# One reading of w_out: block sums in the conv output's place, and the first left sum kept in SBUF

## The chip, the cores and the metric

The kernel runs on one core of a Trainium2 chip. The metric is the device time of one execution in microseconds. Engines are named as in the profile: PE is TensorE (matmul), PEld its weight load, DVE is VectorE, ACT is ScalarE, POOL is GpSimd, SP is SyncE, which issues nearly all of the DMAs and issues them in order. "wo" is the program's name for the PSUM banks of the product with w_out.

## What is computed

One layer of a hybrid decoder: batch 1, 1024 tokens, width 1024, all in fp32. The part that matters here is its middle:

```
c   = silu(layer_norm(conv(...)))
y_b = c @ w_proj_conv
g_a, g_b = split(sigmoid(g + gate_b))
x   = x + (g_a * y_a + g_b * y_b) @ w_out        # w_out is 1024 x 1024
h   = rms_norm(x) * ffn_norm_w
x   = x + (silu(h @ w_gate) * (h @ w_up)) @ w_down
```

The attention branch gives y_a ahead of this. With m = g_a * y_a + g_b * y_b, the stage that is changed is x + m @ w_out, together with the projection with w_proj_conv just before it, in which m is made.

## The kernel before

**Precision.** Each fp32 operand is split into a high part (a cast on ScalarE, `split_hi`, L120) and a low part (a subtraction on VectorE, `split_lo`, L125). A product takes three matmuls: high x high, high x low, low x high. Weights come through `wraw` (two buffers of 128x1024) into `whi` and `wlo` (three buffers of each). A `Stream` (`ws`) holds the list of the loads and splits; `ws.next()` hands out the next weight and sees to it that up to two more are begun.

**The product with w_out.** It is done in seven products of half size, not eight, in Winograd's form of Strassen's method. m is cut into four blocks: token half by even or odd 128-row tile of the contraction. w_out is cut in four: W11, W12, W21, W22, by the even or odd 128-row tile (first digit) and by column half (second digit). The sums are

```
left:   S1 = m21 + m22    S2 = S1 - m11    S3 = m11 - m21    S4 = m12 - S2
right:  T1 = W12 - W11    T2 = W22 - T1    T3 = W22 - W12    T4 = W21 - T2
```

and the products are 11 (m11 W11), 12 (m12 W21), S2 T2, S1 T1, S4 W22, S3 T3, 22 (m22 T4). A product has four contraction tiles j, four row tiles i and three matmuls for each, 48 matmuls of 128x128 by 128x512. They go into three groups of four PSUM banks called a, b and c. Group b (two `pm`, two `pg` banks) takes 11, S2, S3 and 22 one on top of the other. Group a takes 12, group c takes S1 and then S4; a and c use the same four `pw` banks. After each product VectorE adds its banks to the rows of x (`xa`, L1786), which are loaded by `x_rows` (L1744), and only then may a bank be written again.

**Where the operands come from.** In the conv projection (loop over groups of channel tiles `(0,1,2), (3,4), (5,6), (7,)`, token half `sb`, channel tile c) every turn loads a gate (`gt<-g_d`, L1619, eight slots) and a row block of the attention branch (`ya`, L1672), multiplies (L1674), adds (L1675) and splits the result into `mT_hi`, `mT_lo` (all but the block m21, whose place stays empty). After each odd c in the second half, `side_sums` (L552 to L558) makes the four left sums of a pair of channel tiles and stores them in HBM (`so`). Between the turns `weight_sums` (L533 to L544) loads w_out in pieces of 128x512 (2 x 256 columns of two row tiles), makes the four right sums of each piece with four subtractions of 128x256 (L539 to L542) and stores them in HBM (`to`). In the w_out stage the S-products load a left sum and its right operand side by side into one 128x1024 buffer, and split both at once (`ld_seven`: L447, L449, L452); the others load two blocks of w_out or T4 (`ld_two`, L500). The buffers of S2, S1 and S4 are rows of the two large tiles that held the conv output (`rooms`, tags xhi and xlo), which are free once the last conv matmul has read them; the rest goes through `wraw`.

**What sets the order.** Each engine and each DMA queue works in order. The order is made by the framework's planner, which simulates the program with estimated durations and puts what it expects to be ready first, by the order of the program. `with after(ins)` puts what follows behind `ins` on the queue of its engine. So the loads of the S2, S1 and S4 operands and of the x rows stand behind the last DMA issued on SP at that point:

```
            if z == 0 and j == 0:
                with after(last_of(mybir.EngineType.SP)):
                    for step in wo_steps["S2"]:
                        step.load()
                    x_rows(0)
                    for step in wo_steps["S1"]:
                        step.load()
                    x_rows(1)
```

The norm weights of the channel mixer (`fnw_b`, L1703) are loaded by ScalarE's queue and scaled on VectorE (L1732) in the same stage. The transposes of the first token half's normed rows (`norm2`) go in between the matmuls of the last two products, and write into the large tiles (`h2_hi`, `h2_lo`).

Of the kernel before, what the change touches and what calls it, by code (L numbers as in the profile page):

```python
# [57 lines left out]
def kernel(  # L58
# [224 lines left out]
    def wraw():  # L283
        return wp.tile([P, 1024], F32, tag="wraw", name=nm("wraw"), bufs=2)
# [104 lines left out]
    so = {z: [dr.tile([P, 512], F32, name=f"so{z}_{j}") for j in range(NKT // 2)] for z in SIDES[3:]}  # L389
    to = {z: [dr.tile([P, 512], F32, name=f"to{z}_{j}") for j in range(NKT // 2)] for z in SUMS}  # L390
# [46 lines left out]
    WSEVEN = tuple(SEVEN[z] for z in (0, 1, 2, 3, 5, 4, 6))  # L437

    def ld_seven(n, sides, w, sums, raw_tile, which=SEVEN):


        def step(a_, b_, j):
            raw = []

            def load():
                raw.append(raw_tile())
                nc.sync.dma_start(raw[0][:, :512], sides[a_][j][:])  # L447
                if b_ in sums:
                    nc.sync.dma_start(raw[0][:, 512:], sums[b_][j][:])  # L449
# [12 lines left out]
        return [step(a_, b_, j) for a_, b_, _, _, _ in which for j in range(n)]  # L462
# [26 lines left out]
    def ld_two(b_, q):  # L489

        def go():
            raw = wraw()
            for e in range(2):
                j = 2 * q + e
                if b_ in to:
                    src = to[b_][j][:]
                else:
                    r0 = (2 * j + b_[0]) * P
                    src = wout[r0 : r0 + P, 512 * b_[1] : 512 * (b_[1] + 1)]
                nc.sync.dma_start(raw[:, 512 * e : 512 * (e + 1)], src)  # L500
            hi, lo = wsplit(raw)
            return hi[:].rearrange("p (k c) -> p k c", c=512), lo[:].rearrange("p (k c) -> p k c", c=512)

        return go

    rooms = []

    def wo_raw():
        if rooms:
            return rooms.pop(0)  # L510
        return wraw()

    wo_steps = {}
    for e_ in WSEVEN:
        if e_[0][0] == "S":
            wo_steps[e_[0]] = ld_seven(NKT // 2, so, wout, to, wo_raw, (e_,))
        else:
            wo_steps[e_[0]] = [ld_two(e_[1], q) for q in range(2)]
        ws.plan(wo_steps[e_[0]])
# [29 lines left out]
    def side_sums(a11, a21, a12, a22, s1, dst, s3=None):  # L549
# [7 lines left out]
        for z, t_ in (("S1", s1), ("S2", a11), ("S4", a21)):  # L557
            nc.sync.dma_start(dst[z], t_[:])  # L558
# [908 lines left out]
    yp_ctx = ExitStack()  # L1467

    def y_tiles(n):
        yp = yp_ctx.enter_context(tc.tile_pool(name=f"yp{n[0]}", bufs=1, side="right", reuse_waits="tile"))  # L1470
        return lambda name: [
            [yp.tile([P, S], F32R, tag=f"y{z}{k}", name=f"{name}{z}{k}") for k in n]
            for z in ("h", "l")
        ]
# [182 lines left out]
    def wo_tiles():  # L1657
        b = bs.tile([P, 2, 2, 256], F32, tag="wd", name=nm("wd"), bufs=2)
        return [b[:, 0], b[:, 1]]

    osum = weight_sums(NKT // 2, wout, to, wo_tiles, 256)
    osum[0][0]()
    M = {}
    nturn = 0
# [72 lines left out]

    for z, tag in enumerate(("xhi", "xlo")):
        room = f32(big.tile([P, NKT, S], F32R, tag=tag, name=f"room{z}")[:])
        rooms.extend(room[:, k, :] for k in range(NKT if z == 0 else 4))  # L1740
# [7 lines left out]
    for z, (z_, b_, s_, (l, c), full) in enumerate(WSEVEN):  # L1748
        if z == 5:
            h2_hi = big.tile([P, NKT, S], F32R, tag="xhi", name="h2_hi")  # L1750
            h2_lo = big.tile([P, NKT, S], F32R, tag="xlo", name="h2_lo")
# [3 lines left out]
        for j in range(4):  # L1755
            if z_[0] == "S" or j % 2 == 0:
                hi, lo = ws.next()
            if z == 0 and j == 0:
                with after(last_of(mybir.EngineType.SP)):
                    for step in wo_steps["S2"]:  # L1760
                        step.load()
                    x_rows(0)
                    for step in wo_steps["S1"]:
                        step.load()
                    x_rows(1)
                    for step in wo_steps["S4"]:
                        step.load()
            for i in range(4):
                t_ = slice(i * P, (i + 1) * P)
                if z_[0] == "S":  # L1770
                    A, B = [m_[:, t_] for m_ in (hi, lo)], [m_[:, 512:] for m_ in (hi, lo)]
                else:
                    k, cs = 2 * j + int(z_[1]) - 1, TOK[int(z_[0]) - 1]
                    A, B = [m_[k][:, cs][:, t_] for m_ in (mT_hi, mT_lo)], [m_[:, j % 2, :] for m_ in (hi, lo)]
# [284 lines left out]
```

## Time and profile before

| what | value |
|---|---|
| median of 3 runs | 1753.03 us (1752.62 to 1755.97) |
| the profiled execution | 1756.5 us |
| its span on the core | 1754.7 us |
| TensorE busy in the span | 1726.1 us, 98% |
| VectorE, ScalarE, GpSimd busy | 1284.9, 864.1, 210.7 us |
| mean granted TensorE clock | 0.994 |
| HBM read, written | 184.99 MB, 86.54 MB |

The profile is of one execution. Its span runs from the first to the last instruction on the core, and the rows below give times from the span's start. In the rows of groups the numbers are: count, busy us in total, mean ns of one, idle us of the engine before them and what ended that idle time. In rows of the timeline: start, duration, engine, line, operation. In the chain of waits: start, duration, what the time went to. "DMA share" is the mean busy share of 16 DMA engines. The conv projection lies at about 924 to 1013 us, the w_out stage at 1013 to 1106 us.

### The profile page before, as it was taken

The numbers are of one execution on the slowest core, as the hardware profiler recorded it, in microseconds if no ns is written. First come the engines' busy times: TensorE is split into PE (matmuls) and PEld (weight loads), VectorE is DVE, ScalarE is ACT, GpSimd is POOL, SyncE is SP. The second block draws the span as 40 slices with busy tenths as digits, with TensorE's granted clock in tenths as the row PEclk, the third lists the DMA queues.
The fourth block names the chain that finished last, engine by engine and source line by source line (L and its number), as shares of the span: only waits on it lengthen the run. The fifth ranks groups of instructions, "written<-read, shape, count | busy, mean of one in ns | idle before, by whom it ended". The sixth has DMA issues, their size and how long they took to land.

```text
span 1754.7 us, 26010 instructions
## 1 busy us (share of the span) xinstructions
PE 1726.1 (98%) x9245; PEld 1482.7 (84%) x9245; DVE 1284.9 (73%) x2156; ACT 864.1 (49%) x1956; POOL 210.7 (12%) x199
## 2 busy tenths in 40 slices
PE   9999999999999999999999989999999999999999
PEld 7997889998998999987787867788888888888887
DVE  7575889998987988886777756967667666565544
ACT  5333435677776786755465224643333333333332
POOL 4987851000000000000000000000000000000000
PEclk9999999999999999999999989999999999999999
DMA  6343455234244344335855894334545544598663
GB/s 204 115 132 115 156 177 162 75 103 149 81 121 139 105 112 124 115 112 182 298 193 162 276 336 162 108 102 155 169 150 162 179 152 143 165 352 294 216 216 132
DMA packets 267591, 289.52 MB, mean 165 GB/s; under 512 B 17282, under 2 KB 187330, under 8 KB 267460
## 3 DMA queue, kind: packets, MB, share of 16 engines
q1 hardware_dynamic: 265184, 281.08, 50.0%
q0 software_dynamic: 1840, 5.19, 1.0%
q8 instruction: 73, 1.20, 0.3%
q10 hardware_dynamic: 436, 1.58, 0.2%
q14 instruction: 58, 0.48, 0.1%
HBM read 184.99 MB, written 86.54 MB: 155 GB/s over the span
## 4 chain that ended last, share of the span: by engine, by line
PE 85%; DVE 6%; DMA 5%; ACT 2%; issue 1%; SPq 0%; DVEq 0%; ACTq 0%
PE acc L977 29%; PE acc L482 12%; PE pg L168 10%; PE pg L169 10%; PE pg L170 10%; PE sc L1286 2%; PE sc L1285 2%; PE wo L1776 2%; PE pT L1324 2%; DVE acc L596 1%; PE pW L169 1%; PE pW L168 1%; PE pW L170 1%; DMA soS<-gt 1%; PE pg L1103 1%
## 5 line engine op out<-in xcount | busy, mean ns | idle before, releaser
L596 DVE SCALAR_TENSOR_TENSOR acc<-u,cw,acc 128x1023 f32<-128x1023 f32 (+14 forms) x240 | 303.5, 1265 | 12.5 <-ACT acc L590 10.0
L168 PE MATMUL pg<-whi,hT_hi 128*128 128x256 f32 x704 | 199.9, 285 | 0.5 <-DVE v L125 0.5
L170 PE MATMUL pg<-whi,hT_lo 128*128 128x256 f32 x704 | 199.8, 284 | 0.0
L169 PE MATMUL pg<-wlo,hT_hi 128*128 128x256 f32 x704 | 199.4, 284 | 0.0
L125 DVE TENSOR_TENSOR wlo<-draw,whi 128x1024 fp32r<-128x1024 f32 x75 | 91.8, 1223 | 84.1 <-ACT whi L120 76.5
L120 ACT CAST whi<-draw 128x1024 fp32r<-128x1024 f32 x75 | 79.1, 1055 | 129.5 <-PE acc L482 117.6
L120 ACT CAST whi<-wraw 128x1024 fp32r<-128x1024 f32 x98 | 102.9, 1052 | 77.7 <-PE pg L169 33.7
L168 PEld LDWEIGHTS pg<-whi,hT_hi 128*128 128x128 f32 x704 | 133.9, 191 | 2.2 <-DVE v L125 0.7
L169 PEld LDWEIGHTS pg<-wlo,hT_hi 128*128 128x128 f32 x704 | 134.2, 191 | 1.8
L170 PEld LDWEIGHTS pg<-whi,hT_lo 128*128 128x128 f32 x704 | 134.2, 191 | 1.7
L482 PE MATMUL acc<-wlo,whi 128*128 128x512 f32 x308 | 119.8, 389 | 0.0
L482 PE MATMUL acc<-whi,wlo 128*128 128x512 f32 x308 | 119.8, 389 | 0.0
L125 DVE TENSOR_TENSOR wlo<-wraw,whi 128x1024 fp32r<-128x1024 f32 x83 | 102.3, 1234 | 19.2 <-ACT whi L120 18.6
L168 PE MATMUL pg<-hT_hi,whi 128*128 128x512 f32 x288 | 114.5, 398 | 0.1
L169 PE MATMUL pg<-hT_lo,whi 128*128 128x512 f32 x288 | 114.1, 396 | 0.0
L170 PE MATMUL pg<-hT_hi,wlo 128*128 128x512 f32 x288 | 113.7, 395 | 0.0
L1292 ACT ACTIVATE E<-E,mn 128x640 f32<-128x640 f32 (+7 forms) x128 | 99.7, 779 | 23.1 <-DVE mn L1287 22.6
L120 ACT CAST whi<-s 128x1024 fp32r<-128x1024 f32 x54 | 56.8, 1052 | 107.6 <-PE acc L977 103.8
L1287 DVE CUSTOM_DVE_ANT_0 E<-sc,tb 128x512 f32<-128x512 f32 (+3 forms) x128 | 74.2, 585 | 27.6 <-PE pT L1324 13.7
L977 PE MATMUL acc<-h_hi,whi 128*128 128x512 f32 x240 | 93.4, 389 | 0.0
L977 PE MATMUL acc<-h_lo,whi 128*128 128x512 f32 x240 | 93.4, 389 | 0.0
L977 PE MATMUL acc<-h_hi,wlo 128*128 128x512 f32 x240 | 90.1, 389 | 0.0
(349 smaller groups left out, 4583.6 us busy)
## 6 DMA issues: line engine op xcount, KB each, us to landing
wraw<-in_w_gate_up_dram SPq DMA_DIRECT2D x44, 512.0 KB, 4.8
wraw<-in_w_in_dram SPq DMA_DIRECT2D x40, 512.0 KB, 4.6
qs<-qs SPq DMA_DIRECT2D x96, 128.0 KB, 2.3
wd<-in_w_down_dram SPq DMA_DIRECT2D x44, 256.0 KB, 3.2
tdT<-wd SPq DMA_DIRECT2D x88, 128.0 KB, 4.7
draw<-sdS SPq DMA_DIRECT2D x44, 256.0 KB, 3.7
draw<-tdT SPq DMA_DIRECT2D x44, 256.0 KB, 3.9
wraw<-in_w_in_dram SPq DMA_DIRECT2D x32, 256.0 KB, 3.3
```

Of the source, the lines that this page charges most:

```text
L120: act.copy(dst, src)
L125: last_lo[0] = dve.tensor_tensor(dst, src, f32(hi), op=ALU.subtract).ins
L168: pe.matmul(o, lh, rh, start=start, stop=False)
L169: pe.matmul(o, lh, rl, start=False, stop=False)
L170: last_mm[0] = pe.matmul(o, ll, rh, start=False, stop=stop).ins
L482: m = pe.matmul(o[s_][i][:], l_[:, ts], r_[:, 512:], start=start and j + y_ == 0, stop=j == n - 1 and y_ == 2, skip_group_check=not start,)
L596: dve.scalar_tensor_tensor(a_, us[c][:, : S - n], cw[:, c, t : t + 1], a_, op0=ALU.mult, op1=ALU.add)
L977: last_mm[0] = pe.matmul(o[:], a_[x_][:, k, :], b_[y_][:, k, :], start=start and k + x_ + y_ == 0, stop=k == 3 and x_ == 1, skip_group_che ...
L1285: pe.matmul(o[:, :w], qh[:, qs], k, start=True, stop=False)
L1286: last_mm[0] = pe.matmul(o[:, :w], ql[:, qs], k, start=False, stop=True).ins
L1287: dve.tensor_tensor_reduce(e[:, ks], o[:, :w], tb[:, S - nk + c0 : S - nk + c0 + w], 1.0, mn[:, j : j + 1] if c0 else 3.0e38, ALU.add, ALU ...
L1292: act.activation(e[:, :nk], e[:, :nk], AF.Exp, bias=mn[:, j : j + 1], scale=-1.0, accum_out=l[:, j : j + 1])
```

## The change

Five things change, all in these two stages.

1. `weight_sums` for w_out leaves the conv projection, with its tiles, its loads, its subtractions and its stores; `to` is gone.
2. `side_sums` no longer stores S1. The conv projection splits it at once into the empty place of m21 in `mT_hi` and `mT_lo`, and the S1 product takes its left operand there.
3. At the start of the w_out stage W21, W12, W11 and W22 are loaded in one piece (`wload`, 16 loads of 128x512) into rows of the large tiles, behind the last DMA of the conv projection on SP; then the x rows of the first half, S2 and S4 (`sload`), the x rows of the second half, and S3. W11 for the first product is loaded as before, through `wraw` (`ld_first`).
4. The right sums are made in those places by VectorE (`wless`): T1 over W11, T2 in the place beside S2, T3 over W12; T4 goes to the places of m's tiles 0 and 2, once the products that read them are done. The left sums S2, S4, S3 are loaded beside their right operands, and each pair is split as before.
5. The order of the products becomes 11, 12, S1, S2, S4, S3, 22 (before: 11, 12, S2, S1, S4, S3, 22).

The core of the diff:

```diff
-    WSEVEN = tuple(SEVEN[z] for z in (0, 1, 2, 3, 5, 4, 6))
+    WSEVEN = tuple(SEVEN[z] for z in (0, 1, 3, 2, 5, 4, 6))
...
+    def ld_first(q):
...
+            for e in range(2):
+                r0 = 2 * (2 * q + e) * P
+                nc.sync.dma_start(raw[:, 512 * e : 512 * (e + 1)], wout[r0 : r0 + P, 0:512])
+            return wsplit(raw)
...
+    ws.plan([ld_first(q) for q in range(2)])
+    for z_, n_ in (("12", 2), ("S1", 2), ("S2", 4), ("S4", 4), ("S3", 4), ("22", 2)):
+        ws.plan([lambda k_=(z_, j): wsplit(room[k_]) for j in range(n_)])
...
         for z, t_ in (("S1", s1), ("S2", a11), ("S4", a21)):
-            nc.sync.dma_start(dst[z], t_[:])
+            if z in dst:
+                nc.sync.dma_start(dst[z], t_[:])
...
-    osum = weight_sums(NKT // 2, wout, to, wo_tiles, 256)
-    osum[0][0]()
...
-                nturn += 1
-                if nturn % 2 == 0:
-                    with after(last_of(mybir.EngineType.DVE)):
-                        if len(osum) > 1:
-                            osum[1][0]()
-                        osum.pop(0)[1]()
+                    split_hi(mT_hi[c - 1][:, cs], s1[:])
+                    split_lo(mT_lo[c - 1][:, cs], s1[:], mT_hi[c - 1][:, cs])
...
+    for z, n in (("12", 2), ("S1", 2), ("S2", 4), ("S4", 4), ("S3", 4)):
+        for j in range(n):
+            room[z, j] = raws.pop(0)
...
+    def wless(z, a_, b_):
+        for j in range(4):
+            dve.tensor_tensor(wblock(z, j), wblock(a_, j), wblock(b_, j), op=ALU.subtract)
...
+        if z == 0:
+            with after(last_of(mybir.EngineType.SP)):
+                wload("12", (1, 0))
+                wload("S3", (0, 1))
+                wload("S1", (0, 0))
+                wload("S4", (1, 1))
+                x_rows(0)
+                sload("S2")
+                sload("S4")
+                x_rows(1)
+                sload("S3")
+        if z == 1:
+            wless("S1", "S3", "S1")
+            wless("S2", "S4", "S1")
+        if z == 3:
+            for q in range(2):
+                room["22", q] = f32(yps[0].tile([P, S], F32R, tag=f"yh{2 * q}", name=f"T4_{q}")[:])
+            wless("22", "12", "S2")
+            wless("S3", "S4", "S3")
```

More of the change, by code (lines that the diff above doesn't have):

```diff
@@ L388 @@
     td = {z: [dr.tile([P, 512], F32, name=f"td{z}_{j}") for j in range(NFF // 2)] for z in SUMS}
[L389 to L390 removed]
+    so = {z: [dr.tile([P, 512], F32, name=f"so{z}_{j}") for j in range(NKT // 2)] for z in SIDES[3:] if z != "S1"}
     b_d = dr.tile([H, TL], F32, name="b_d")
@@ L435, with ld_seven @@
     )
-    WSEVEN = tuple(SEVEN[z] for z in (0, 1, 2, 3, 5, 4, 6))
-    def ld_seven(n, sides, w, sums, raw_tile, which=SEVEN):
+    WSEVEN = tuple(SEVEN[z] for z in (0, 1, 3, 2, 5, 4, 6))
+    def ld_seven(n, sides, w, sums, raw_tile):
         def step(a_, b_, j):
@@ L460, in step @@
             return go
-        return [step(a_, b_, j) for a_, b_, _, _, _ in which for j in range(n)]
+        return [step(a_, b_, j) for a_, b_, _, _, _ in SEVEN for j in range(n)]
     def seven(n, stream, bank, add, soon):
@@ L487, in seven @@
                         add(l, i, c, o[s_][i], full)
-    def ld_two(b_, q):
+    room = {}
+    def ld_first(q):
         def go():
```

68 lines of the change are left out of this document (24 added, 44 removed).

## The prediction

> **What bounds the kernel now.** I read the page first, then TensorE's waits between 840 and 1190 us, then busy times by stretch, then the chain of waits, then the SP queue.
>
> ```profile
> span 1754.7 us, 26010 instructions
> ...
> PE 1726.1 (98%) x9245; PEld 1482.7 (84%) x9245; DVE 1284.9 (73%) x2156; ACT 864.1 (49%) x1956; POOL 210.7 (12%) x199
> ```
>
> TensorE is the bound and the change gives it no matmul less, so the change is worth only what it does to the gaps on TensorE. Those near it, as TensorE's waits (us in total, times, longest):
>
> ```profile
> PE wo L1776 <- DVE xa L1786: 4.7, 2, 4.4
> PE wo L1776 <- DVE gt L1674: 3.9, 1, 3.9
> ...
> PE pg L170 <- DVE wlo L125: 1.5, 1, 1.5
> PE pg L168 <- ACT whi L120: 1.4, 1, 1.4
> ...
> PE wo L1776 <- DVE r L671: 0.7, 1, 0.7
> ```
>
> Two sit inside the w_out products (`wo`), one before them for 3.9 us and one for 4.4; the pair of 1.4 and 1.5 is at 949 to 954 us, in the conv projection. The stretches show where they lie and what follows them:
>
> ```profile
> core 0: us, PE busy (x) PEld busy (x) DVE busy (x) ACT busy (x) POOL busy (x), PEclk, DMA share, GB/s
> ...
> 946.50:954.50 8.00, 4.97 (x20) 3.19 (x20) 6.84 (x13) 4.41 (x6) 0.00 (x0) 1.00 0.60 154
> 954.50:1013.00 58.50, 58.50 (x260) 48.42 (x259) 43.48 (x76) 15.11 (x22) 0.00 (x0) 1.00 0.87 271
> 1013.00:1023.00 10.00, 6.14 (x28) 4.77 (x27) 2.98 (x6) 2.18 (x4) 0.00 (x0) 1.00 0.79 265
> 1023.00:1027.00 4.00, 4.00 (x12) 3.17 (x11) 3.93 (x7) 1.57 (x2) 0.00 (x0) 0.57 0.99 324
> 1027.00:1040.00 13.00, 13.00 (x59) 10.76 (x58) 4.76 (x6) 2.10 (x2) 0.00 (x0) 1.00 1.04 365
> 1040.00:1045.00 5.00, 0.65 (x3) 0.21 (x3) 1.52 (x3) 1.04 (x1) 0.00 (x0) 0.90 1.03 404
> 1045.00:1051.00 6.00, 5.99 (x15) 4.71 (x16) 5.28 (x8) 2.63 (x7) 0.00 (x0) 0.52 1.03 419
> ```
>
> After each long gap the granted clock is about half: 0.57 over 4 us costs 4 x 0.43 = 1.7 us, 0.52 over 6 us costs 2.9; the shorter gaps at 950 are followed by a clock of 1.00. So the gaps are worth 2.9 us in the conv projection, 3.9 + 1.7 = 5.6 us at the first w_out product, 4.4 + 2.9 = 7.3 us at the third, 0.7 at the last: 16.5 us, the most that the change can give. The DMA engines are at 0.87 to 1.04 in all this time: here DMA sets the order. The chain of waits says which transfers:
>
> ```profile
> 1011.41 5.12 DMA soS<-gt
> 1016.55 0.32 SPq L1619
> ...
> 1026.19 6.12 DMA soS<-gt
> 1032.33 3.94 DMA room<-soS
> 1036.36 6.95 DMA fnw_b<-in_ffn_norm_w_dram
> 1043.44 0.69 DVE fnw_b L1732
> 1044.17 0.70 DVE xa L1786
> 1045.01 24.43 PE wo L1776 x94
> ```
>
> The first gap: the last gate load (L1619) needs a slot that a store of a left sum holds. The store was issued only at 1011.41, and the SP queue's own waits and ScalarE's say why and what it did:
>
> ```profile
> SPq L533 <- DMA toT<-wd: 7.9, 4, 4.5
> ...
> SPq L1619 <- DMA soS<-gt: 5.2, 2, 4.2
> ```
> ```profile
> ACT gt L1620 <- DMA gt<-g_d: 13.8, 1, 13.8
> ```
>
> L533, the load of w_out for the block sums, waits 4.5 us in one place for the stores of earlier sums, and all behind it on SP waits too. The second gap is the x rows and the norm weights (fnw_b), which came after a backlog of 24 loads of sides and sums.
>
> **The change part by part.** T is the start of the first w_out product. The rate of a product, from the starts of 23 matmuls:
>
> ```profile
> 1012.96 0.39 PE L1776 MATMUL wo<-whi,mTh 128*128 128x512 f32 x1
> ...
> 1017.95 0.39 PE L1776 MATMUL wo<-wlo,mTh 128*128 128x512 f32 x1
> ```
>
> 22 steps in 4.99 us are 0.227 us each; a product of 48 takes 10.9 us. Products are due at T, T+10.9, T+21.8, T+32.7 and so on.
>
> *Block sums out of the conv projection.* Gone: 16 loads of 256 KB, 32 stores of 128 KB, 32 subtractions, and 4 stores of S1; added there: 4 casts and 4 subtractions that split S1.
>
> ```profile
> L539 DVE TENSOR_TENSOR wd<-wd 128x256 f32<-128x256 f32 x8 | 3.3, 418 | 0.6 <-DMA toT<-wd 0.6
> ...
> L554 DVE TENSOR_TENSOR s<-gt,gt 128x512 f32<-128x512 f32 x4 | 2.7, 686 | 0.0
> ```
>
> VectorE loses 32 x 0.42 = 13.4 us and gains 4 x 0.69 = 2.8. From 954.5 to 1013 TensorE never stops, so this pays only at the edges. At 950 the casts and subtractions of two weights wait for their slots, not for DMA; without two chunk subtractions between them I take -0.3 us, ends 0 and -2.9. At the first product: 9.4 MB less traffic, and no load on SP that waits for a store. The left sums of channels 4 and 5 need a product that ends three turns (16 us) before T; sums, store (5.1 by the chain) and gate load leave some 4 us. I take the gap as gone: -5.6, ends 0 and -5.6.
>
> *w_out read in one piece, second product.* All 16 loads go on SP behind its last instruction, the store of S4 of the last pair. VectorE's time from the last gated product to that sum:
>
> ```profile
> 1021.46 0.68 DVE L1674 TENSOR_TENSOR gt<-pg,gt 128x512 f32<-128x512 f32 x1
> ...
> 1025.84 0.69 DVE L556 TENSOR_TENSOR gt<-gt,gt 128x512 f32<-128x512 f32 x1
> ```
>
> That is 5.1 us with a weight's low part (1.2) between, which cannot stand there now: 3.9. So the store goes out at T+4.1 and the loads from T+4.2. Issue, landing, and the rows for cast, low part and additions:
>
> ```profile
> 1022.89 0.43 SPq L449 DMA_DIRECT2D room<-toT  x1
> ```
> ```profile
> L500 SPq DMA_DIRECT2D wraw<-in_w_out_dram x8: 333/454/591, 983.6 to 1017.9; - x8
> ...
> DMA to landing us min/median/max: 3.1/4.2/5.6
> ```
> ```profile
> L1786 DVE TENSOR_TENSOR xa<-wo,xa 128x512 f32<-128x512 f32 x28 | 17.8, 681 | 0.1
> ...
> L125 DVE TENSOR_TENSOR wlo<-room,whi 128x1024 fp32r<-128x1024 f32 x12 | 14.4, 1220 | 19.9 <-ACT whi L120 19.9
> ...
> L120 ACT CAST whi<-room 128x1024 fp32r<-128x1024 f32 x12 | 12.4, 1052 | 30.0 <-PE wo L1776 24.1 <-DMA room<-soS 6.0
> ```
>
> The second load is issued at T+4.65 and lands at T+7.8 to 8.9; cast at T+9.9, low part at T+11.2 at the latest; due T+10.9 and T+11.1. The norm weights' DMA is on ScalarE's queue and waits for the last store (6.1 us in the chain: T+10.2); if the cast stands behind it, it ends at T+11.3. I take +0.3, ends 0 and +1.5 (landing at 5.6).
>
> *S1 moved to third place, fed by the sums made in place.* T1 needs 12 loads of 262 KB at 404 GB/s (0.65 us each, the stretch at 1040): T+4.2+7.8, and 2.4 for the landing (3.1 less one transfer) is T+14.4. Four subtractions of 0.69, cast and low part end by T+19.4; due T+21.8, so the work hides, by 2.4 us. T2 is due at T+32.7, T3 and T4 later: their 12 subtractions (8.3 us) lie in VectorE's idle time under the products (4.76 busy of 13 us at 1027). T4's place is free once S1's product has read it, 33 us before it is due. Two splits of 128x1024 fewer (S1 needs 2, not 4).
>
> But S1 is summed in the banks of the second product (both are on `pw`; before, S2 stood between them). It waits until VectorE has added the first bank to x, and in VectorE's order the four additions of the first product stand ahead, so until the fourth x row is there. Ahead of it on the DMA engines: two last stores 0.52 MB, w_out 4.19, norm weights 0.52, four x rows 2.10, in all 7.34 MB from T+4.1; at 404 GB/s 18.2 us, and 2.4 to land: T+24.7. Two additions (0.68, then 0.6 in a row of them): T+26.0, against T+22.1 with the 0.3 above: a gap of 3.9 us, which cost 1.7 of clock the other time: 5.6 us. The old gap of 7.3, for the same rows, goes: -1.7. Ends: no gap (-7.3), and 271 GB/s, the slowest rate at a DMA share of 0.87: 27.1 us, T+34.9, 12.8 + 2.9 = 15.7, so +8.4.
>
> The rate decides that term, so a rule on it is weighed. Rows: 404 and 419 GB/s while loads from HBM landed in SBUF. The Trainium skill, "DMA: Bandwidth & Descriptors", section "Where 436 GB/s comes from", says that HBM limits a core's HBM-SBUF transfers to about 358 GB/s. By that rule the x row comes 2.3 us later and the sum below would be -5.7; the trace, at 404 to 419 for 11 us, does not agree.
>
> *Sides, later x rows.* S2's sides (1.05 MB) land by T+27.3, S4's and the second x rows by T+35.1 (3.1 MB more at 404); S2 is due at T+32.7 and the banks of S1 are needed again at T+43.6, all later still by the gap. Nothing is on the path.
>
> *Last products.* Before, S3's and T4's operands came through two buffers:
>
> ```profile
> L120 ACT CAST whi<-wraw 128x1024 fp32r<-128x1024 f32 x11 | 11.6, 1052 | 7.0 <-DMA wraw<-toT 4.7 <-PE wo L1776 1.3 <-DMA wraw<-in_w_gate_up_dram 0.9
> ```
>
> The 4.7 us of waiting goes, VectorE is ahead, and the 0.7 us gap at the last product goes with it: -0.7, ends 0 and -0.7.
>
> **Sum.** -0.3 - 5.6 + 0.3 - 1.7 - 0.7 = -8.0 us. The profiled execution took 1756.5 us (span 1754.7), 3.5 over the median 1753.03 of the runs; against the median this is 1745.0 us.
>
> **The rivals.**
> 1. All the gaps go, because the x rows come in time (before T+20) and the planner closes the gap at 950. For it: SP is free of waits, fewer bytes. Against it: 7.3 MB stand before the fourth row. -16.5 us: 1736.5.
> 2. The gate load stays late. Only VectorE's and ScalarE's orders, not SP's stores, would hold it (it came 8.5 us after the product's end: 1021.46 - 1012.96). Then the 5.6 us stay, and the loads start 8.5 us later: second product's low part at T+19.7 against T+16.7, gap 3.0; the additions T+34.5 against T+30.4, 4.1 + 1.7. In all 14.4 against 12.9, less 1.0 for the rest: +0.5, 1753.5.
> 3. Slower: the x rows behind w_out come late. It decides when, with the gate late as in 2, the rate falls below 346 GB/s (3 us more on 18.2, and 0.2% is passed). At the 324 GB/s of the stretch from 1023 the 7.34 MB take 22.7 us, 4.5 more: +5.0, 1758. For it: 265 to 365 GB/s before 1040. Against it: those stretches had SP waiting; 16 loads in a row at 0.43 us could feed 600 GB/s.
> 4. VectorE's order puts the additions of the first product ahead of T1's subtractions. Then the cast of T1 ends at T+27.6, the low part at T+28.8; a gap of 6.4 + 2.9 = 9.3, so +2.0 in that term in place of -1.7: -4.3, 1748.7. It counts with the forecast.
>
> **How the numbers follow.** About 0.2% (3.5 us) is what a measurement tells from no change. Forecast with rival 4: 0.48; rival 1: 0.22; rival 2: 0.16; rival 3: 0.14. Faster 0.48 + 0.22 = 0.70, the same 0.16, slower 0.14. The range runs from near rival 1 (1737) to between rivals 2 and 3 (1756); the likeliest case's own is 1741 to 1749.
>
> **What would show it.** In the profile after: no wait of `wo` for L1674, and a clock of 1.00 through the first two products; a wait of the third product for `xa`, of about 4 us with a dip behind it; the first x row's addition near T+22; DMA share below 0.6 from 960 to 1010. The prediction is wrong if the gate load of the last channel still lands after T, if the second product waits for w_out by more than 1.5 us, or if T1's subtractions come behind the x rows.

## The result

The changed kernel takes 1740.33 us (median of 5 runs, 1738.83 to 1742.1) against 1752.62 us before: a ratio of 0.9934, 95% interval 0.9914 to 0.9955. That is faster, by 12.3 us where 8.0 were forecast. The profiled execution of after took 1740.33 us itself; that of before, 1756.5, lay 3.9 over its median, so the pair of profiles shows 16.2 us.

The page of the changed kernel, its first lines:

```profile
span 1738.6 us, 25865 instructions
...
PE 1718.4 (99%) x9245; PEld 1480.4 (85%) x9245; DVE 1283.3 (74%) x2142; ACT 865.4 (50%) x1958; POOL 210.8 (12%) x199
```

TensorE's waits between 840 and 1190 us (us in total, times, longest):

```profile
PE wo L1785 <- DVE xa L1795: 2.3, 1, 2.3
...
PE pg L168 <- DVE gt L1654: 1.5, 1, 1.5
PE wo L1785 <- ACT whi L120: 1.1, 1, 1.1
```

The wait for the gated product (L1674 before, L1654 now) is gone from `wo`. In the conv projection, at 948 to 950 us, one wait of 1.5 us, for another gated product, stands where before had the pair of 1.4 and 1.5. The wait of 4.4 us for the x rows is a wait of 1.1 at the third product. The 2.3 are new: they stand ahead of the last product. The stretches, with the columns and nearly the bounds of the prediction's rows:

```profile
946.50:954.50 8.00, 6.47 (x29) 5.01 (x29) 6.84 (x10) 4.61 (x7) 0.00 (x0) 1.00 0.48 145
954.50:1013.00 58.50, 58.50 (x260) 48.45 (x259) 39.21 (x58) 18.57 (x27) 0.00 (x0) 1.00 0.59 195
1013.00:1023.00 10.00, 10.00 (x46) 8.29 (x45) 5.88 (x9) 3.15 (x3) 0.00 (x0) 1.00 1.00 348
1023.00:1027.00 4.00, 4.00 (x19) 3.33 (x18) 4.00 (x6) 0.87 (x1) 0.00 (x0) 1.00 1.05 407
1027.00:1040.00 13.00, 11.88 (x53) 9.55 (x52) 11.06 (x17) 3.92 (x10) 0.00 (x0) 1.00 1.03 414
1040.00:1045.00 5.00, 5.00 (x24) 4.14 (x23) 3.04 (x5) 1.06 (x1) 0.00 (x0) 1.00 0.98 378
1045.00:1051.00 6.00, 6.00 (x28) 4.99 (x27) 4.76 (x6) 3.06 (x3) 0.00 (x0) 1.00 0.02 7
```

The reader is to see three things. The DMA share from 954.5 to 1013 fell from 0.87 to 0.59. TensorE is busy in all 10 us from 1013 (6.14 before), and the granted clock is 1.00 in every row where before had 0.57 and 0.52. And the transfers are over by 1045, where before still moved 419 GB/s.

Where the time lies follows from three starts in each kernel, taken from TensorE's timeline. Of before, the first matmul of the conv projection (the first of `wo`, 1012.96, and that of the third product, 1045.01, stand in the prediction):

```profile
921.94 0.40 PE L168 MATMUL pg<-cT_hi,whi 128*128 128x512 f32 x1
```

Of after, the same three:

```profile
920.66 0.40 PE L168 MATMUL pg<-cT_hi,whi 128*128 128x512 f32 x1
...
1009.57 0.39 PE L1785 MATMUL wo<-whi,mTh 128*128 128x512 f32 x1
...
1032.61 0.47 PE L1785 MATMUL wo<-whi,mTh 128*128 128x512 f32 x1 [1.12 <-ACT whi L120]
```

From the conv projection's first matmul to T (the first w_out product) it is 91.0 us before and 88.9 after; from T to the start of the third product 32.1 and 23.0. Together that is 123.1 and 111.9: 11.2 us. The two profiles differ by 16.2. Of the rest, 1.3 us lie ahead of the conv projection (it starts at 921.94 and at 920.66), in code that the change leaves alone, and 3.7 behind the start of the third product, where before has the slow clock that the prediction puts at 2.9.

What SP issued after T, from its timeline (start, duration of issue, line, count):

```profile
1009.54 3.65 SPq L1731 DMA_DIRECT2D room<-in_w_out_dram  x8
1013.29 0.38 SPq L543 DMA_DIRECT2D soS<-gt  x1
1013.71 1.27 SPq L1731 DMA_DIRECT2D room<-in_w_out_dram  x2
1016.24 0.33 SPq L543 DMA_DIRECT2D soS<-gt  x1
1016.83 3.80 SPq L1731 DMA_DIRECT2D room<-in_w_out_dram  x6
1020.95 1.58 SPq L1735 DMA_DIRECT2D room<-soS  x3
1022.92 2.26 SPq L1743 DMA_DIRECT2D xa<-in_x_dram  x4
```

The x rows are issued at T+13.4; before it was T+24.0, as SP's timeline of before has it:

```profile
1036.98 6.68 SPq L1744 DMA_DIRECT2D xa<-in_x_dram  x8
```

And the loads of w_out begin at T itself, eight of them ahead of the two last stores of left sums, not behind these. The section on the change says that they stand behind the last DMA of the conv projection; this trace shows that they don't. In the program, `last_of` returns the last instruction of any kind on SP, which need not be a DMA; r4 below asks for the last DMA, and there they do stand behind the stores.

VectorE's timeline of after around the third product:

```profile
1022.28 1.29 DVE L1739 TENSOR_TENSOR room<-room,room 128x512 f32<-128x512 f32 x2 [0.57 <-DMA room<-in_w_out_dram]
...
1024.63 0.69 DVE L1739 TENSOR_TENSOR room<-room,room 128x512 f32<-128x512 f32 x1
...
1028.84 0.69 DVE L1739 TENSOR_TENSOR room<-room 128x512 f32<-128x512 f32 x1
1029.45 1.22 DVE L125 TENSOR_TENSOR wlo<-room,whi 128x1024 fp32r<-128x1024 f32 x1
1030.58 3.07 DVE L1795 TENSOR_TENSOR xa<-wo,xa 128x512 f32<-128x512 f32 x5
```

The first addition to x comes at T+21.0 (before T+31.2), behind a low part with no idle time between. The third product starts 0.15 us after the third addition of this row, so this and not the cast named in its row ended the wait.

It was not the x rows that held these additions back. The first x row, issued at 1022.92, took 5.7 us to land (T+19.1), and the third landed at T+21.6. What stands ahead of the additions on VectorE without a pause is its own work: from T1's last subtraction (T+13.3), which follows on a wait for a block of w_out, a low part, the eight subtractions for T2 and T3 (1024.63 to 1029.5, of which T3's are due three products later), and another low part.

### The profile page after: what moved, and what is told of

It reads as the page before. It is cut to its first block, busy times and chain, and to the rows that moved or that the text cites. A ratio compares the mean times of both kernels' runs of the same rounds, so it can differ in the third digit from the quotient of the medians.

```text
span 1738.6 us, 25865 instructions
## 1 busy us (share of the span) xinstructions
PE 1718.4 (99%) x9245; PEld 1480.4 (85%) x9245; DVE 1283.3 (74%) x2142; ACT 865.4 (50%) x1958; POOL 210.8 (12%) x199
## 4 chain that ended last, share of the span: by engine, by line
PE 89%; DVE 4%; DMA 3%; ACT 2%; POOL 1%; issue 1%; SPq 0%; POOLq 0%; ACTq 0%; DVEq 0%
PE acc L962 28%; PE acc L481 12%; PE pg L168 11%; PE pg L169 11%; PE pg L170 11%; PE wo L1785 3%; PE sc L1271 2%; PE sc L1270 2%; PE pT L1309 2%; DVE acc L581 1%; PE pW L169 1%; PE pW L168 1%; PE pW L170 1%; PE pg L1088 1%; PE pQ L797 1%
## 5 line engine op out<-in xcount | busy, mean ns | idle before, releaser
L581 DVE SCALAR_TENSOR_TENSOR acc<-u,cw,acc 128x1023 f32<-128x1023 f32 (+14 forms) x240 | 303.5, 1265 | 15.9 <-ACT acc L575 13.4
L120 ACT CAST whi<-wraw 128x1024 fp32r<-128x1024 f32 x90 | 94.5, 1052 | 76.3 <-PE pg L169 38.9
L125 DVE TENSOR_TENSOR wlo<-wraw,whi 128x1024 fp32r<-128x1024 f32 x75 | 92.6, 1237 | 15.5 <-ACT whi L120 14.7
L1272 DVE CUSTOM_DVE_ANT_0 E<-sc,tb 128x512 f32<-128x512 f32 (+3 forms) x128 | 74.2, 585 | 26.7 <-PE pT L1309 13.1
L962 PE MATMUL acc<-h_hi,wlo 128*128 128x512 f32 x240 | 90.2, 389 | 0.0
```

What stands on the lines that cost most here:

```text
L120: act.copy(dst, src)
L125: last_lo[0] = dve.tensor_tensor(dst, src, f32(hi), op=ALU.subtract).ins
L581: dve.scalar_tensor_tensor(a_, us[c][:, : S - n], cw[:, c, t : t + 1], a_, op0=ALU.mult, op1=ALU.add)
L962: last_mm[0] = pe.matmul(o[:], a_[x_][:, k, :], b_[y_][:, k, :], start=start and k + x_ + y_ == 0, stop=k == 3 and x_ == 1, skip_group_che ...
L1272: dve.tensor_tensor_reduce(e[:, ks], o[:, :w], tb[:, S - nk + c0 : S - nk + c0 + w], 1.0, mn[:, j : j + 1] if c0 else 3.0e38, ALU.add, ALU ...
```

## The experiments

Theories at the start. A: SP's order decides, the block sums' loads held everything behind them. B: the bytes decide, the DMA engines are full and the x rows come when the traffic ahead is moved. C: S1 in third place, fed from SBUF, is the cause by itself. All kernels run beside the kernel before. The ratio is to the runs of the kernel before in the same group of runs, whose medians are 1751.9 to 1753.3 us, so the ratios compare better than the medians. The table has, beside it, two lengths from each profile: conv projection's first matmul to T, and T to the start of the third product, both worked out from starts as above. The last column takes the two lengths, which are of one execution, from the median of the runs.

| kernel | median us | ratio, 95% interval | conv | T to third | both | median less both |
|---|---|---|---|---|---|---|
| before | 1752.6 | | 91.0 | 32.1 | 123.1 | 1629.5 |
| after | 1740.3 | 0.9934 (0.9914 to 0.9955) | 88.9 | 23.0 | 111.9 | 1628.4 |
| r12, after again | 1741.3 | 0.9938 (0.9925 to 0.9950) | 89.8 | 22.9 | 112.6 | 1628.7 |
| r1 | 1751.8 | 0.9997 (0.9989 to 1.0006) | 89.7 | 31.9 | 121.6 | 1630.2 |
| r2 | 1750.5 | 1.0000 (0.9990 to 1.0010) | 92.4 | 26.8 | 119.2 | 1631.3 |
| r3 | 1750.9 | 0.9993 (0.9985 to 1.0002) | 90.2 | 31.2 | 121.4 | 1629.5 |
| r4 | 1746.1 | 0.9968 (0.9956 to 0.9980) | 89.3 | 27.5 | 116.8 | 1629.3 |
| r5 | 1740.9 | 0.9935 (0.9922 to 0.9947) | 88.9 | 22.0 | 110.9 | 1630.0 |
| r6 | 1747.3 | 0.9973 (0.9961 to 0.9985) | 92.2 | 27.4 | 119.6 | 1627.7 |
| r7 | 1741.0 | 0.9931 (0.9917 to 0.9945) | 88.9 | 22.8 | 111.7 | 1629.3 |
| r8 | 1740.9 | 0.9923 (0.9910 to 0.9935) | 89.0 | 23.2 | 112.2 | 1628.7 |
| r9 | 1749.0 | 0.9974 (0.9963 to 0.9984) | 90.6 | 30.5 | 121.1 | 1627.9 |
| r10 | 1745.8 | 0.9955 (0.9942 to 0.9967) | 89.4 | 26.4 | 115.8 | 1630.0 |
| r11 | 1739.8 | 0.9928 (0.9916 to 0.9940) | 89.2 | 21.8 | 111.0 | 1628.8 |

The last column is 1627.7 to 1631.3 for all fourteen, while the medians differ by 12.8: the difference between any two of these kernels lies ahead of the third product's start, but for 3.6 us at most and mostly 1 or 2. The two ends are r6 and r2, which reach the third product at the same point (119.6 and 119.2 us): r2 has a wait of 2.3 us at the last product, r6 has none over 0.3.

### r1: before, with the block sums' DMAs on another queue

The loads and stores of `weight_sums` for w_out (L533, L544) go on GpSimd's queue; all else is the kernel before.

```diff
-                        nc.sync.dma_start(
+                        queue.dma_start(
...
-    osum = weight_sums(NKT // 2, wout, to, wo_tiles, 256)
+    osum = weight_sums(NKT // 2, wout, to, wo_tiles, 256, nc.gpsimd)
```

> The kernel before, but the 16 loads and 32 stores of the w_out block sums in the conv projection are issued by GpSimd's queue and no longer by SP. Bytes and VectorE work are the same. Theory (order on the SP queue): the left-sum stores and gate loads no longer stand behind loads that wait for stores, so TensorE's gap of 3.9 us before L1674's release and its slow clock (1.7 us) go, ratio to the kernel before 0.995 to 0.998. Rival (bytes): 8.4 MB more on the DMA engines are the cause, the gap stays within 1 us, ratio 0.999 to 1.001.

Measured: 0.9997. TensorE's waits in r1:

```profile
PE wo L1776 <- DVE xa L1786: 10.3, 2, 9.9
...
PE pg L168 <- DVE gt L1674: 1.5, 1, 1.5
```

and the x rows on SP's timeline and VectorE's first additions:

```profile
1034.45 6.51 SPq L1744 DMA_DIRECT2D xa<-in_x_dram  x8
...
1041.49 1.42 DVE L1786 TENSOR_TENSOR xa<-wo,xa 128x512 f32<-128x512 f32 x2 [4.89 <-DMA xa<-in_x_dram]
```

The first gap of 3.9 us is gone, as theory A has it, but the time is the rival's, and the wait at the third product grew from 4.4 to 9.9 us: given back. `wo` ran on through two products, but the x rows were still issued at T+24.0 and added from T+31.0 (before: T+24.0, T+31.2). A is right about the first gap and wrong about the time: closing a gap ahead of another that hangs on a transfer only moves the wait.

### r2 and r3: after, with the block sums put back beside it

The changed kernel, which also makes and stores the block sums in the conv projection as before, on SP (r2, shown here) or on GpSimd's queue (r3, with nc.gpsimd in the first line). The sums are not read: this is extra work, with 4.2 MB more read from HBM and 4.2 more written.

```diff
+    osum = weight_sums(NKT // 2, wout, to, wo_tiles, 256, nc.sync)
+    osum[0][0]()
+    nturn = 0
...
+                nturn += 1
+                if nturn % 2 == 0:
+                    with after(last_of(mybir.EngineType.DVE)):
+                        if len(osum) > 1:
+                            osum[1][0]()
+                        osum.pop(0)[1]()
```

> The changed kernel with the block sums of w_out put back into the conv projection, on SP as before; nothing reads them. It tells what leaving them out is worth by itself. Theory: the gap at the first w_out product comes back by 2 to 6 us, and the w_out loads start later, so 4 to 9 us over the changed kernel: ratio to the kernel before 0.9955 to 0.999. Rival (the whole gain is made in the w_out stage): ratio stays at 0.993 to 0.994.

> As the last one, with the same loads, stores and subtractions, but on GpSimd's queue. Theory (order on SP): next to no loss against the changed kernel, ratio to the kernel before 0.993 to 0.995. Rival (bytes, or VectorE's 13 us): as bad as with the sums on SP, 0.9955 to 0.999.

Measured: 1.0000 and 0.9993. The block sums eat the whole gain on either queue, more than any of the expectations gave them. TensorE's waits in r2:

```profile
PE wo L1799 <- DVE xa L1809: 7.2, 2, 4.9
...
PE pg L170 <- DVE wlo L125: 1.5, 1, 1.5
PE pg L168 <- ACT whi L120: 1.4, 1, 1.4
```

The pair of 1.5 and 1.4 us in the conv projection, which before had, is back, and the wait for the x rows is 4.9 us. In r3, with SP free of the sums, the x rows were nevertheless issued at T+24.0, behind all twelve loads of left sums, and the first addition came at T+30.4, for a wait of 8.4. So for the whole gain the sums have to go, and which queue they use is not what costs. What the two runs do not separate is how the sums do it: by their bytes, or by where the planner puts the x rows when they are there.

### r9 and r10: the x rows forced forward

r9 is the kernel before with the four x rows put on SP right behind S2's loads, ahead of S1's and S4's; r10 is r3 with them right behind the loads of w_out. What stood between follows behind, in its order.

```diff
+                    with after(last_dma()):
+                        x_rows(0)
+                    with after(last_dma()):
...
```

> The kernel before with one thing changed: on SP the four first x rows stand behind the loads of S2 and ahead of those of S1 and S4, whatever the planner expects. Bytes are the same. Theory (TensorE waits at the third product until x rows come, and what stands ahead of them on the DMA engines sets when): the first addition moves from T+31 to between T+24 and T+28, the gap there shrinks by 3 to 5 us with its slow clock, ratio 0.995 to 0.998. Rival (the place of the x rows is held by the stores of the last block sums until T+23 or so, and the last S2 sum comes late too): x rows as late as before, ratio 0.999 to 1.001.

> The changed kernel with the unused block sums back, on GpSimd's queue (ratio 0.9993 by itself, first addition to x at T+30.4, TensorE's gap there 8.4 us), and with the first four x rows put right behind the 16 w_out loads on SP. Theory (the planner's later place for the x rows made the loss, not bytes or VectorE's work): first addition at T+24 to T+27, gap 3 to 5 us, ratio 0.995 to 0.9975. Rival (8.4 MB more traffic, or the place held by the sums' stores): first addition still past T+29, ratio 0.999 to 1.0.

Measured: 0.9974 and 0.9955. In r9 the first gap stays (4.05 us) and the wait at the third product falls to 2.6; the first addition comes at T+29.6, later than the T+24 to T+28 expected: the x rows, placed further forward, were still issued only at T+21.4, and the first took 8.1 us to land. Ahead of it VectorE stands idle for 8.5 us until the norm weights come, which were issued just before the x rows, and for 1.0 more until the first x row does. In r10 the x rows are issued from T+15.4 on and added from T+24.3, the wait falls from 8.4 to 3.8 us, and of the 0.0055 in the ratio between r3 and r12 0.0038 come back. So the place of the x rows on SP is worth over half, with the sums' traffic still there.

The rest, 3.5 us at the third product, comes by another way. T1's last subtraction starts at T+13.1 in r12 and at T+16.6 in r10, because the blocks of w_out land later: the first load, issued at T in r10, took 6.9 us to land, where the load issued at T+0.4 in r12 took 2.9. From that subtraction to the first addition it is 7.7 us in both, filled by the subtractions for T2 and T3 and two low parts. In r10 the first x row had landed by then (T+22.6).

### r4: after, with the loads of w_out truly behind the last store

`last_dma` finds the last DMA issued on SP, the store of the last pair's S4.

```diff
-            with after(last_of(mybir.EngineType.SP)):
+            with after(last_dma()):
```

> The changed kernel with the 16 w_out loads put behind the store of the last S4 sum, which is the place that the prediction gave them; measured, 8 of them went out ahead of the last two stores, 0.1 us before T. Theory: the loads start at T+4.1 and the fourth x row lands near T+25, the second product waits up to 1.5 us, S1 waits 2 to 5 us, clock dip possible: 3 to 7 us over the changed kernel, ratio to the kernel before 0.995 to 0.9975. Rival (the planner's bank-by-bank order of S1 hides the later x rows too): within 1.5 us of the changed kernel, ratio 0.993 to 0.994.

Measured: 0.9968, 1746.1 us; the prediction, which was made for this order, says 1745.0. VectorE's subtractions and first additions and TensorE's third product in r4 (T is 1010.03):

```profile
1025.29 2.58 DVE L1744 TENSOR_TENSOR room<-room,room 128x512 f32<-128x512 f32 x4 [0.85 <-DMA room<-in_w_out_dram]
...
1034.34 0.68 DVE L1744 TENSOR_TENSOR room<-room 128x512 f32<-128x512 f32 x1
1034.94 4.26 DVE L1800 TENSOR_TENSOR xa<-wo,xa 128x512 f32<-128x512 f32 x7
...
1037.56 0.76 PE L1790 MATMUL wo<-whi,mTh 128*128 128x512 f32 x1 [5.53 <-DVE xa L1800]
```

The first addition comes at T+24.9, the gap is 5.5 us, and the clock falls behind it:

```profile
1037.60:1041.60 4.00, 4.00 (x10) 3.13 (x11) 3.34 (x5) 2.52 (x8) 0.00 (x0) 0.50 1.06 421
```

So most of the 4.7 us between the forecast and the result are the place of these sixteen loads: moving them behind the store costs 4.8 us against r12 and 5.8 against the first measurement of after.

The way it costs is not the one that was forecast. The prediction has the fourth x row at T+24.7, and in r4 it landed there (issued at 1027.21, 7.5 us to land). But the third product did not wait for it: the first three rows had landed by T+23.4, and VectorE works without a pause from 1025.29 to the additions, on the subtractions for T1, T2 and T3 and two low parts. T1's last subtraction starts at T+17.2, and the first addition follows 7.8 us later; in after it is 7.7 (T+13.3 and T+21.0). The later w_out blocks push back VectorE's subtractions, and these the additions.

### r5 and r6: the order of the products, and S1 kept in SBUF

r5 is the changed kernel with the products in the old order; r6 is the kernel before with S1 kept in SBUF: no store and no reload of it, T1 loaded in pairs, block sums and order as before.

```diff
-    WSEVEN = tuple(SEVEN[z] for z in (0, 1, 3, 2, 5, 4, 6))
+    WSEVEN = tuple(SEVEN[z] for z in (0, 1, 2, 3, 5, 4, 6))
```

That was r5. Of r6, where `so` has no S1:

```diff
-            nc.sync.dma_start(dst[z], t_[:])
+            if z in dst:
+                nc.sync.dma_start(dst[z], t_[:])
...
+                    split_hi(mT_hi[c - 1][:, cs], s1[:])
+                    split_lo(mT_lo[c - 1][:, cs], s1[:], mT_hi[c - 1][:, cs])
```

> The changed kernel with the products in the old order (11, 12, S2, S1, S4, S3, 22), all else kept. If the gain hangs on when the x rows and the w_out blocks arrive, the order is worth little: S2's banks are free after the first addition to x, as S1's are, so it starts near T+22 with a gap of 0 to 2.5 us (its sides land near T+21 and need a cast and a low part of 1.0 and 1.2 us), and the ratio to the kernel before stays at 0.993 to 0.9945. If putting S1 third is a cause of the gain by itself, the gap at the third product comes back to 4 us or more and the ratio is 0.996 or higher.

> The kernel before with only the left sum S1 kept in SBUF and split in the conv projection: no store and no reload of S1, T1 loaded in pairs; block sums, loads of w_out and order of the products as before. If the block sums' traffic is what holds back the x rows, this alone gives little: the x rows are issued at the same place, 1 to 1.5 MB less stands ahead of them, the first addition to x comes 0 to 3 us earlier than before (T+31 to T+28), ratio 0.998 to 1.0005. If S1's place is a cause by itself, most of the gain is here: ratio 0.996 or below and a first gap under 2 us.

Measured: 0.9935 and 0.9973. r5 has no gap over 0.3 us at the third product (it starts at T+22.0): the order is worth nothing that can be measured, and theory C falls as far as the order goes. r6 came out between the two expectations. TensorE's only large wait there:

```profile
PE wo L1788 <- DVE xa L1798: 5.4, 1, 5.4
```

Its first gap is gone, though the block sums are still on SP, and the wait at the third product grew by only 1 us: with S1's four stores and four reloads gone the x rows are issued at T+19.5 and added from T+26.5 (before T+24.0 and T+31.2). Keeping S1 is worth some 4.9 us by itself, through the same two places. Its conv projection stays at 92.2 us: that part belongs to the block sums.

### r8 and r11: the x rows ahead of W22, then VectorE's order as well

r8 is the changed kernel with the x rows ahead of W22's loads; r11 also puts the subtractions of T4 and T3 behind S1's additions on VectorE (the last three lines).

```diff
+                with after(last_dma()):
+                    x_rows(0)
+                with after(last_dma()):
+                    wload("S4", (1, 1))
...
+            with after(last_add[0]):
                 wless("22", "12", "S2")
                 wless("S3", "S4", "S3")
```

> The changed kernel with the order on SP fixed: W21, W12, W11, the first four x rows, then W22 and the rest. Theory (TensorE waits for x rows at the third product): the first addition to x moves from T+21 to T+18 or 19 and the gap of 1.3 us at S1 goes, 1 to 1.5 us, ratio 0.9925 to 0.993. Rival (T1's operand or the place of the x rows is late): the gap stays, ratio 0.9934 +- 0.0005, or S2's first matmuls wait for W22 instead.

> The changed kernel with the four x rows of the first half issued ahead of W22, and the subtractions of T4 and T3 put behind S1's additions to x on VectorE (in the run with the x rows early alone, the third product still waited 1.24 us, for additions that stood behind those subtractions and a weight's low parts). Expected: no gap over 0.3 us at the third product, the gap at the last product still there (2.3 us), ratio to the kernel before 0.9915 to 0.9925, 0.5 to 1.5 us below the changed kernel. If it stays at 0.993, the gap of 1 us at the third product is taken up by a later wait.

Measured: 0.9923 and 0.9928. In r8 the first addition comes 5.9 us earlier than in the changed kernel (T+15.1), and the third product still waits 1.24 us and starts no earlier (T+23.2 against T+23.0). VectorE's timeline in r8:

```profile
1028.14 0.68 DVE L1744 TENSOR_TENSOR room<-room,room 128x512 f32<-128x512 f32 x1
1028.74 0.68 DVE L1744 TENSOR_TENSOR room<-room 128x512 f32<-128x512 f32 x1
1029.34 0.68 DVE L1744 TENSOR_TENSOR room<-room,room 128x512 f32<-128x512 f32 x1
1029.94 0.68 DVE L1744 TENSOR_TENSOR room<-room 128x512 f32<-128x512 f32 x1
1030.55 0.68 DVE L1803 TENSOR_TENSOR xa<-wo,xa 128x512 f32<-128x512 f32 x1
```

Four subtractions, two for T2 (the rows that read two tiles) and two for T3 (due three products later), stand ahead of the addition that frees the bank. So the last 1.2 us are VectorE's order, no longer a transfer. In r11, where T3's stand behind, the gap is gone:

```profile
1020.00:1033.00 13.00, 13.00 (x59) 10.78 (x58) 11.16 (x17) 3.85 (x6) 0.00 (x0) 1.00 1.04 408
```

Its time, 1739.8 us, is the lowest median of all, 1.5 below r12 on the same chip; the intervals overlap (0.9916 to 0.9940 and 0.9925 to 0.9950), so a gain over the changed kernel isn't shown; the ratio is just above the 0.9915 to 0.9925 that was expected.

### r7: after, with the norm's multiplications later

The new 2.3 us ahead of the last product. VectorE's timeline of after:

```profile
1074.26 2.74 DVE L1698 SCALAR_TENSOR_TENSOR xa<-xa,r,fnw_b 128x512 f32<-128x512 f32 x4
1076.91 1.22 DVE L125 TENSOR_TENSOR wlo<-T,whi 128x1024 fp32r<-128x1024 f32 x1
1078.05 0.74 DVE L1698 SCALAR_TENSOR_TENSOR xa<-xa,r,fnw_b 128x512 f32<-128x512 f32 x1
1078.71 0.68 DVE L1795 TENSOR_TENSOR xa<-wo,xa 128x512 f32<-128x512 f32 x1
```

Five multiplications of `norm2` and a low part stand ahead of the addition for which the last product waits. r7 puts them behind the additions.

```diff
-            if 0 <= 4 * (z - 5) + j - 3 < 4:
-                with after(last_mm[0]):
-                    norm2(4 * (z - 5) + j - 3, r2[0], tr_first)
+            if z == 6:
+                with after(last_mm[0]), after(last_add[0]):
+                    norm2(j, r2[0], tr_first)
```

> The changed kernel, but VectorE's norm multiplications of the first token half stand behind the four additions of S3. Measured before: the last product waits 2.3 us (a gap of 2.8) for the first of these additions, with three to five norm multiplications of 0.7 us ahead of it on VectorE. Theory (VectorE's order makes this gap): the gap falls below 1 us, the kernel is 1 to 2.5 us shorter than the changed one, ratio to the kernel before 0.992 to 0.993. Rival (the norm is late next): the gaps of 1.4 and 1.0 us at the first matmuls of the channel mixer grow by what is saved, ratio 0.9934 +- 0.0005.

Measured: 0.9931, no change against the changed kernel. The wait at the last product is 0.4 us, and the transposes and the first matmuls behind the stage wait instead:

```profile
1088.40:1096.40 8.00, 4.23 (x21) 2.70 (x20) 7.25 (x17) 7.88 (x17) 0.00 (x0) 0.77 0.69 211
```

TensorE is idle for 3.8 of these 8 us and slower in the rest. VectorE's and ScalarE's work on the norm has to be done before the channel mixer begins; moving it moves the wait.

### r12: the changed kernel beside the last group

> The changed kernel unaltered, on the chip and beside the runs of the kernel before of this group, as the measure for the other three: ratio 0.9934, within its interval (0.9914 to 0.9955).

Measured: 0.9938 (0.9925 to 0.9950), the same as in the first measurement.

## Why the prediction was right, and where it was off

The direction and the range held (1737 to 1756, "faster" at 0.70); the forecast of 1745.0 was 4.7 us too high. Step by step:

- **"Block sums out of the conv projection", -0.3.** Too small. The conv projection took 91.0 us before and 88.9 after. With the block sums on SP it is 90.6 to 92.4 (before, r2, r6, r9), on GpSimd's queue 89.4 to 90.2 (r1, r3, r10), without them 88.9 to 89.8. One wait of 1.5 us is left where there were two, and the end of -2.9 was nearer than the value taken.
- **The first gap, -5.6.** Right: 6.14 busy us of 10 became 10.00, and the clock behind it 1.00. The cause given was only half of it. r1 removes the gap by moving the sums off SP, r6 by S1's stores alone with the sums still there: either will do, and r1 shows that this gap alone is worth nothing, since the next wait takes it. Adding the gaps up as if each were its own was the weak point of the sum; it worked here because the additions to x came earlier too.
- **Second product, +0.3.** Didn't come: W21's loads went out at T, so its first cast ran at 1014.08 (T+4.5), where T+10.9 was due. Nor does it wait in r4, where the loads begin only at T+5.2.
- **"S1 moved to third place", -1.7.** This is the step that failed, in two ways. First, it put all sixteen loads "behind its last instruction, the store of S4", hence "from T+4.1"; they ran from T. The gap was 1.28 us at a clock of 1.00, not 3.9 with 1.7 behind it: 4.3 us, nearly all of the 4.7. r4, with the loads behind that store, is the check: 1746.1 us for 1745.0. Second, it named the wrong wait. It has the third product wait for the fourth x row, because "the four additions of the first product stand ahead", and puts the subtractions for T2 and T3 into "VectorE's idle time". The traces show otherwise. The third product started behind the third addition in after and the fourth in r4, so the four of the first product did not all stand ahead; the x rows that were needed had landed before the first addition; and the subtractions for T2 and T3 stood right ahead of it, so that it came 7.7 to 7.8 us after T1's last subtraction in after, r12, r4 and r10 alike. r8 bears it out: x rows added 5.9 us earlier did not start the third product earlier. That r4's first addition, at T+24.9, lies so near the forecast T+24.7, and its time so near 1745.0, is in part luck; the third product there started at T+27.5, where T+26.0 was due. In before, where VectorE stood idle and the first x row landed just ahead of the first addition (1044.05 and 1044.17), the prediction read the wait rightly.
- **"Last products", -0.7.** Wrong: VectorE is not ahead there. The wait became 2.3 us (0.7 before); in return the waits behind the stage, 2.8 us in all in before, are 1.7 in after. Together that is 0.5 us lost, not 0.7 gained, and r7 shows that the two trade against each other.
- **The rate.** The prediction weighed the 358 GB/s that the Trainium skill gives in "DMA: Bandwidth & Descriptors" against rows of 404 and 419. After shows 407 and 414 in loads from HBM once the stream runs, but 348 from 1013 to 1023. In r4 the step worked out with 404 gave the landing of the fourth x row rightly, by two errors that nearly cancel: the loads began 1 us later than worked out, and the 0.52 MB of norm weights were not ahead of it. The Trainium skill, "HBM Reference", section "Specifications (TRN2)", says that a core that streams alone measures well above that share, about 425; the rows above 400 agree with this, for this kernel runs on one core.
- **What would show it.** No wait of `wo` for L1674, clock 1.00 through the first two products, DMA share 0.59 and below: as foretold. The first addition "near T+22" came at T+21.0, but with 1.1 us of waiting and no dip.

What stays open: whether the block sums hold the transfers back through their bytes or through the places that the planner gives the loads when the sums are there. r10 shows that the place of the x rows is worth over half. Its slower landing of w_out loads issued at T speaks for the bytes in the rest, but a kernel with the same bytes and exactly the same order of all other loads wasn't run; nor was the changed kernel with only T2's and T3's subtractions moved.

The norm weights were loaded at 1036.36 in before and at 945.89 in after. They come behind T in every kernel that makes the block sums (T+15 to T+23) and at 945 to 948 us in every one that doesn't. VectorE's idle time ahead of the additions ended with them in before (4.3 us), r6 (3.8) and r9 (8.5), but in all three the first x row landed 0.7 to 1.7 us later still. What they can have cost is then their own traffic ahead of the x rows, an estimated 1.3 us for 0.52 MB at 404 GB/s. Why they come earlier without the sums, and what that is worth, wasn't tried.

## What to carry to other kernels

Gaps in a row that hang on the same stream of transfers do not add: ask of each what the next one waits for, and count only the shift of the last (here the start of the third product gave every median to within 2 us). Ask it again once the transfer comes earlier: here the wait then passed to VectorE, whose order put work that was due later ahead of the additions that freed the bank. Read off the place of a moved load from what the queue would issue, not from the line in the source that orders it: "behind the last instruction" was 4 us off, and that was most of the error of the forecast. Extra traffic ahead of a stage cost as much on one queue as on the other, because operands of the stage came later.

## What was not expected of the hardware

The slow clock behind a gap does not grow with the gap. Behind an idle time of 9.9 us, r1:

```profile
1042.40:1046.40 4.00, 4.00 (x10) 3.13 (x11) 3.93 (x7) 1.61 (x5) 0.00 (x0) 0.50 1.02 416
1046.40:1050.40 4.00, 4.00 (x19) 3.29 (x18) 1.04 (x2) 1.28 (x4) 0.00 (x0) 1.00 1.03 408
```

Behind one of 3.8 us, in r10:

```profile
1035.50:1039.50 4.00, 4.00 (x10) 3.14 (x11) 3.33 (x6) 2.26 (x7) 0.00 (x0) 0.50 1.06 407
1039.50:1043.50 4.00, 4.00 (x15) 3.25 (x14) 1.60 (x2) 1.35 (x3) 0.00 (x0) 0.76 1.03 410
```

The long gap lost 4 x 0.50 = 2.0 us of clock, the short one 2.0 + 4 x 0.24 = 3.0; in r3, behind 8.4 us, it was 0.64 over 4 us and then 1.00, a loss of 1.4. Behind the single waits of 1.1 and 1.5 us in after (1013 to 1051 and 946 to 954 above) the clock stayed at 1.00. In between it went both ways: behind the pair of 1.4 and 1.5 us in the conv projection it was 1.00 in before and 0.57 over the next 4 us in r2. The wait of 2.3 us ahead of the last product was followed by this in after,

```profile
1079.50:1083.50 4.00, 3.96 (x18) 3.32 (x19) 4.00 (x7) 2.14 (x7) 0.00 (x0) 1.00 0.34 133
```

and by this in r11, for the same instructions (in r12, the very kernel of after, by 0.57):

```profile
1079.40:1083.40 4.00, 4.00 (x11) 3.21 (x12) 4.00 (x7) 2.14 (x7) 0.00 (x0) 0.60 0.37 142
```

The Trainium skill, "TensorE: Matmul & The Clock Gate", section "Part 1: The HAM clock gate", has a window of about 3.4 us that runs freely: half the clock after an idle one, the full clock after a busy one. A loss that doesn't grow with the gap agrees with that, and so does one kernel's going both ways. The rule that the same part gives, no idle gaps over about 3.4 us, is not safe here: the wait of 2.6 us in r9 was followed by a clock of 0.57 over 4 us. The prediction's 1.7 and 2.9 us for its two gaps are two values out of a spread, 1.4 to 3.0 us behind the waits of 2.6 us and more at the first and third products, in which the length of the wait doesn't show.
